# Expert loop: a sixth pair of weight buffers, one result instruction, and a new order of the steps around the weight splits

## The chip, the cores and the metric

One Trainium2 chip, one of its cores, one launch of one program. The metric is the device time of the kernel in microseconds. The engines are called PE (TensorE), DVE (VectorE), ACT (ScalarE), POOL (GpSimd) and SP (SyncE, which only issues DMAs here).

## The reference

One layer of a latent diffusion backbone: 1024 latent tokens and 256 context tokens of width 1024, fp32. Modulated RMSNorm, one combined projection, grouped and differential attention, an output projection with a gated residual; then modulated RMSNorm, a mixture of 32 experts, four for each token, a gated residual and a last RMSNorm. The change is in the experts. For the rows of an expert `e`, with `gate` each row's softmax weight among its four experts, and `gt2` the residual's gate:

```
hcat  = xb @ w_in[e] + b_in[e]                       # 1024 -> 2048
x_glu = min(hcat[:, :1024], 7)
x_lin = clip(hcat[:, 1024:], -7, 7)
act   = x_glu * sigmoid(1.702 * x_glu) * (x_lin + 1)
y     = act @ w_out[e] + b_out[e]                    # 1024 -> 1024
x    += gt2 * sum over a token's experts of gate * y
```

## The kernel before, in words

The program computes modulation, attention and routing in its first 918 us, then runs `stage_e`, the 32 experts, then adds up and normalises. All of it is one unrolled program; each engine works through its own queue in the order in which the code issues the instructions, and waits at an instruction until what that reads or overwrites is ready. The expert stage is issued by hand in a fixed order (`manual_schedule`).

Each expert has up to 128 main rows and up to 64 leftover rows. The products are done in three matmuls on split operands: a weight `w` becomes `wh` (ScalarE's copy, rounded to TensorE's fp32r) and `wl = w - wh` (VectorE), the rows likewise, and `mm3` (lines 87 to 89) adds `xh*wh + xh*wl + xl*wh`. The unit is a weight half, 128 x 1024: two column blocks of 512, so six matmuls. An expert has 16 halves for the input product (`in_mm`, i = 0 to 15, even i for the first 1024 columns of `H`) and eight for the output product (`out_mm`, k = 0 to 7). The split halves lie in a ring of NW = 5 pairs `wh`, `wl` (lines 1197 and 1198): after each half, `split_ahead(1)` issues the split of the half that stands NW places further on in the list `seq`, into the pair that was just used.

PSUM has eight banks: `H` four, `y` two (one tile each), and two ring tiles `r` that serve everything else: the transposes of rows (`columns`, line 1185), of activations (`act_cols`, line 1292), the leftover input (`L[e]`, two of them, blanked by ScalarE at line 1170) and the leftover output. A ring tile is handed on when its last reader is done.

Iteration `e` of the main loop runs in this order:

- issue the gathers of expert e+1 (POOL, main rows and leftovers);
- the input phase, 16 halves. Behind the split that follows a half: `result(e-2)` at i = 1, the activations of e-1 transposed at i = 3, 5, 7 (`act_cols`), the two leftover tiles blanked at i = 11;
- `act_a`: clamp and gelu of `H`'s first half, clamp of its second (lines 1261 to 1263); `left_in`: a branch on the expert's count (line 1225, 1227), and behind it the leftover rows' input product, on raw weights (line 1249); the loads of expert e+1's input weights (SP); `act_l`: clamps of the two leftover tiles (lines 1270, 1271);
- the output phase of expert e-1, eight halves. Behind the split that follows: the rows of e+1 transposed at k = 1 and 3, the leftovers' at k = 4 (`columns`), a blank tile for the leftover output at k = 5, the products of the activation at k = 6 (`act_b`, lines 1277, 1278);
- `left_out`: the leftover output of e-1, behind the same branch; the loads of the output weights of e.

`result` (lines 1338 and 1342) scales each bank of `y` by gate and `gt2` into `o`, the leftovers into `ol`, and POOL scatters them with addition into DRAM (lines 1344, 1349). For the last expert the products come at k = 3 and its activations are transposed at k = 5, 6, 7, since no input phase follows. Lines 1104 and 1114 issue the weight loads; nine buffers of 1 MB hold input rows, four hold output rows.

Of the kernel before, what the change touches and what calls it, by code (L numbers as in the profile page):

```python
# [20 lines left out]
D = 1024  # L21
# [27 lines left out]
class K:  # L49
# [1029 lines left out]
    def stage_e(self):  # L1079
# [4 lines left out]
        with ExitStack() as ctx:  # L1084
# [7 lines left out]
            NW = 5  # L1092
# [25 lines left out]

            def gather(e):
                gather_main(e)  # L1120
                gather_left(e)
# [134 lines left out]
            COLS, KB, ACI, RI, LB, KAB = (1, 3, 4), 5, (3, 5, 7), 1, 11, 6  # L1256

            def act_a(e):
                gm = sp.tile([128, D], F32, name="ga", tag="ga", bufs=1)
                ln = sp.tile([128, D], F32, name="ln", tag="ln", bufs=1)  # L1260
                nc.vector.tensor_scalar(gm, H[e][:, :1024], 7.0, None, op0=OP.min)
                nc.scalar.activation(gm, gm, AF.Gelu_apprx_sigmoid)
                nc.vector.tensor_scalar(ln, H[e][:, 1024:], 7.0, -7.0, op0=OP.min, op1=OP.max)
                A[e] = [gm, ln]

            def act_l(e):
                gm = sp.tile([128, 2, 256], F32, name="gal", tag="gal", bufs=1)
                ln = sp.tile([128, 2, 256], F32, name="lnl", tag="lnl", bufs=1)
                for u in range(2):
                    nc.vector.tensor_scalar(gm[:, u], L[e][u][:, :256], 7.0, None, op0=OP.min)  # L1270
                    nc.vector.tensor_scalar(ln[:, u], L[e][u][:, 256:], 7.0, -7.0, op0=OP.min, op1=OP.max)
                nc.scalar.activation(gm, gm, AF.Gelu_apprx_sigmoid)
                AL[e] = [gm, ln]

            def act_b(e):
                gm, ln, gl, ll = A[e] + AL[e]
                nc.vector.scalar_tensor_tensor(gm, ln, 1.0, gm, op0=OP.add, op1=OP.mult)  # L1277
                nc.vector.scalar_tensor_tensor(gl.rearrange("p u c -> p (u c)"), ll.rearrange("p u c -> p (u c)"), 1.0,
                                               gl.rearrange("p u c -> p (u c)"), op0=OP.add, op1=OP.mult)
# [21 lines left out]
            def out_mm(e, k):  # L1301
                if k == 0:
                    Y[e] = [ps.tile([128, 512], F32, name="y", tag="y", bufs=2) for _ in range(2)]
# [9 lines left out]
            def left_out(e):  # L1313
                ac = ACT[e][2]
                p = Y[e][2]
# [17 lines left out]
            def result(e):  # L1333
                y0, y1, yl = Y.pop(e)
                o = sp.tile([128, D], F32, name="o", tag="o", bufs=1)
                for b, y in enumerate((y0, y1)):
                    c = slice(512 * b, 512 * b + 512)
                    nc.vector.scalar_tensor_tensor(o[:, c], y, self.gm[:, e:e + 1], self.gt2[:, c],  # L1338
                                                   op0=OP.mult, op1=OP.mult)
                ol = sp.tile([128, 2, 256], F32, name="ol", tag="ol", bufs=1)  # L1340
# [45 lines left out]
            columns(0, 1)  # L1386
            for e in range(NE + 1):
                if 0 < e < NE - 1:
                    gather(e + 1)
                for i in range(16 if e < NE else 0):  # L1390
                    in_mm(e, i)
                    if e > 0 or i < 13:
                        split_ahead(1)
                    else:
                        done[1] += 1
                    if i == RI and e > 1:
                        result(e - 2)
                    if i in ACI and e > 0:
                        act_cols(e - 1, ACI.index(i))
                    if i == 0 and e == 0:  # L1400
                        LLS = left_lists()
                    if i == 2 and e == 0:
                        left_lists2(*LLS)
                        gather_left(0)
                        load_out(0, range(2, 4), nc.gpsimd)
                    if i in (9, 10) and e == 0:
                        columns(1, i - 9)
                    if i == 11 and e == 0:
                        columns(0, 2)
                        gather_left(1)  # L1410
                    if i == LB:
                        L[e] = [blank(), blank()]
                if e == NE:
                    result(e - 2)
                if e < NE:
                    act_a(e)
# [5 lines left out]
                if e == 0:  # L1422
                    load_out(0, range(2))
                    act_l(0)
                    split_ahead()
                    columns(1, 2)
                elif e < NE:
                    act_l(e)
                for k in range(8 if e > 0 else 0):
                    out_mm(e - 1, k)  # L1430
                    split_ahead(1)
                    if e < NE:
                        if k in COLS and e + 1 < NE:
                            columns(e + 1, COLS.index(k))
                        if k == (KAB if e < NE - 1 else 3):
                            act_b(e)
                        if e == NE - 1 and k in (5, 6, 7):
                            act_cols(e, (5, 6, 7).index(k))
                    if k == KB:
                        Y[e - 1].append(blank())  # L1440
                if e == 0:
                    act_b(e)
# [174 lines left out]
```

## Time and profile before

| | |
|---|---|
| time, median of 3 runs | 2431.16 us (2431.13 to 2438.26) |
| profiled execution | 2435.69 us, its span 2433.9 us |
| PE busy | 2253.5 us, 93% |
| DVE busy | 1898.0 us, 78% |
| ACT busy | 1507.5 us, 62% |
| POOL busy | 549.8 us, 23% |
| DMA moved | 557.00 MB, mean 229 GB/s |

The expert stage begins at 918 us; its last weight matmul stands near 2395 us. An engine's busy time counts an instruction from its start to its end; instructions of one engine overlap a little, so their pitch (start to start) is shorter than their duration. A matmul's end is modelled, and each lasts longer than its pitch. In a wait, the name behind the arrow is what the profile takes to have ended it; "issue" means that it shows nothing. PEclk is the granted share of TensorE's full clock, 2.4 GHz; the lower level is 1.2 GHz.

### The profile page before, as it was taken

To read this page: it belongs to the slowest core of one execution; us is meant where nothing else is said; L and a number is where in the kernel's file an instruction comes from. 1 tells how busy PE (TensorE), PEld (TensorE's weight loads), DVE (VectorE), ACT (ScalarE), POOL (GpSimd) and SP (SyncE) were. 2 spreads that over 40 slices of the span, in tenths; PEclk is the share of its full clock that TensorE was granted. 3 is DMA by queue.
4 is the path that set the end of the run, shared out by engine and by line. 5 is a ranking of instruction groups with operands and counts; after the bars stand their busy time and mean duration, and the time that the engine had idled before them with its cause. 6 is when DMAs were issued, how large, how long until landed. Compare 5 with 4: busy or idle time off the path is not lost. (4 is left out here: it accounts for less than half of the span.)

```text
span 2433.9 us, 36793 instructions
## 1 busy us (share of the span) xinstructions
PE 2253.5 (93%) x13548; PEld 1760.6 (72%) x13548; DVE 1898.0 (78%) x2987; ACT 1507.5 (62%) x2285; POOL 549.8 (23%) x699
## 2 busy tenths in 40 slices
PE   6999999998999989999999899999999999999993
PEld 3787788887887767776767777667777677677762
DVE  5897067768997768998867898778878888887884
ACT  4321188887887216776656677666667666666762
POOL 3402100001335342221212222122122122122211
PEclk9999999999999988999999999999999999999996
DMA  7546141111003456896878798779779689687875
GB/s 275 186 135 197 58 134 40 35 32 44 23 19 113 170 200 264 331 363 244 331 269 323 268 366 307 289 291 351 270 292 376 247 333 350 248 341 290 303 273 174
DMA packets 133890, 557.00 MB, mean 229 GB/s; under 512 B 18720, under 2 KB 29632, under 8 KB 100880
## 3 DMA queue, kind: packets, MB, share of 16 engines
q1 hardware_dynamic: 103472, 476.21, 51.3%
q0 software_dynamic: 30176, 77.43, 11.4%
q8 instruction: 169, 2.77, 0.5%
q14 instruction: 73, 0.60, 0.1%
HBM read 495.04 MB, written 50.14 MB: 224 GB/s over the span
## 5 line engine op out<-in xcount | busy, mean ns | idle before, releaser
L1197 ACT ACTIVATE wh<-rin 128x1024 fp32r<-128x1024 f32 x520 | 550.4, 1060 | 261.0 <-PE H L89 231.8
L1198 DVE TENSOR_TENSOR wl<-rin,wh 128x1024 fp32r<-128x1024 f32 x520 | 620.0, 1220 | 110.6 <-ACT wh L1197 108.7
L87 PE MATMUL H<-wh,xt 128*128 128x512 f32 x1024 | 415.8, 406 | 0.0
L88 PE MATMUL H<-wl,xt 128*128 128x512 f32 x1024 | 407.8, 398 | 2.7 <-DVE ga L1277 1.5
L89 PE MATMUL H<-wh,xt 128*128 128x512 f32 x1024 | 407.8, 398 | 0.0
L1198 DVE TENSOR_TENSOR wl<-rout,wh 128x1024 fp32r<-128x1024 f32 x248 | 296.4, 1222 | 88.5 <-ACT wh L1197 84.4
L1197 ACT ACTIVATE wh<-rout 128x1024 fp32r<-128x1024 f32 x248 | 256.6, 1054 | 46.8 <-PE H L89 27.3
L89 PEld LDWEIGHTS H<-wh,xt 128*128 128x128 f32 x1024 | 194.7, 190 | 48.8 <-issue 2.6
L88 PEld LDWEIGHTS H<-wl,xt 128*128 128x128 f32 x1024 | 195.1, 191 | 43.5 <-DVE wl L1198 1.0
L87 PEld LDWEIGHTS H<-wh,xt 128*128 128x128 f32 x1024 | 194.9, 190 | 42.6 <-issue 0.7
L87 PE MATMUL y<-wh,at 128*128 128x512 f32 x512 | 210.7, 411 | 0.0
L88 PE MATMUL y<-wl,at 128*128 128x512 f32 x512 | 202.8, 396 | 0.5 <-DVE wl L1198 0.5
L89 PE MATMUL y<-wh,at 128*128 128x512 f32 x512 | 203.1, 397 | 0.0
L1126 POOL DMA_INDIRECT xg<-h2d,im x31 | 33.2, 1070 | 659.4 <-PE r L1185 658.8
L658 ACT ACTIVATE PT<-T 128x512 f32<-128x512 f32 (+1 forms) x256 | 144.8, 573 | 45.5 <-PE T L657 44.6
L657 PE MATMUL T<-ident,P 128*128 128x128 f32 x960 | 147.4, 276 | 9.8 <-DVE P L620 5.5
L1349 POOL DMA_INDIRECT acc<-ol,il x64 | 151.3, 2365 | 17.7 <-DVE wl L1198 15.2
L567 ACT ACTIVATE P<-S,m 128x1024 f32<-128x1024 f32 x128 | 143.4, 1121 | 11.8 <-DVE m L553 6.4
L1344 POOL DMA_INDIRECT acc<-o,im x32 | 51.7, 1615 | 417.3 <-DVE o L1338 385.4
L657 PEld LDWEIGHTS T<-ident,P 128*128 128x128 f32 x960 | 113.0, 141 | 39.6 <-DVE Q L486 9.1
L88 PE MATMUL g<-wl,hh 128*128 128x512 f32 (+1 forms) x368 | 137.4, 373 | 3.5 <-POOL wl L232 3.5
L87 PE MATMUL g<-wh,hh 128*128 128x512 f32 (+1 forms) x368 | 138.8, 377 | 0.5 <-ACT hh L82 0.5
(340 smaller groups left out, 4356.8 us busy)
## 6 DMA issues: line engine op xcount, KB each, us to landing
rin<-in_w_in SPq DMA_DIRECT2D x252, 1024.0 KB
rout<-in_w_out SPq DMA_DIRECT2D x122, 1024.0 KB
ld<-in_w_ada SPq DMA_DIRECT2D x48, 512.0 KB
wr<-in_w_qkv SPq DMA_DIRECT2D x32, 256.0 KB
Q<-Q SPq DMA_DIRECT2D x32, 256.0 KB
xl<-in_x SPq DMA_DIRECT2D x8, 512.0 KB
xr<-in_x SPq DMA_DIRECT2D x8, 512.0 KB
acc<-x POOLq DMA_DIRECT2D x8, 512.0 KB
```

The source lines that it names most:

```text
L87: nc.tensor.matmul(p, ah, bh, start=start, stop=False)
L88: nc.tensor.matmul(p, ah, bl, start=False, stop=False)
L89: nc.tensor.matmul(p, al, bh, start=False, stop=stop)
L567: nc.scalar.activation(parts[k][0], parts[k][1], AF.Exp, bias=m, scale=0.125, accum_out=l2[:, k:k + 1])
L657: nc.tensor.transpose(p[:, k, :], P[:, 128 * j:128 * j + 128], self.ident)
L658: nc.scalar.activation(PT[u - 1][:, 4 * g:4 * g + len(w), :], p[:, :len(w)], AF.Copy)
L1126: nc.gpsimd.indirect_dma_start(out=xg, out_offset=None, in_=self.h2d[:, :], in_offset=bass.IndirectOffsetOnAxis(ap=self.im[:, e:e + 1], ax ...
L1197: nc.scalar.activation(h, src, AF.Copy)
L1198: nc.vector.tensor_tensor(l, src, h.bitcast(F32), op=OP.subtract)
L1344: sc = [nc.gpsimd.indirect_dma_start(out=self.acc[:, :], out_offset=bass.IndirectOffsetOnAxis(ap=self.im[:, e:e + 1], axis=0), in_=o, in_o ...
L1349: i = nc.gpsimd.indirect_dma_start(out=self.acc.rearrange("t (j d) -> (t j) d", j=4), out_offset=bass.IndirectOffsetOnAxis(ap=self.il[:, u ...
```

## The change

Ring of split weights: six pairs instead of five. `y` becomes one tile over two banks, and `result` scales it in one instruction; `o` and `ol` take the slots of `ln` and `lnl`. The steps are cut smaller (`clamp_g`, `gelu`, `clamp_l`, `clamp_left`, `gelu_left`, `act`, `act_left`) and issued by `around_in` and `around_out`, each called before ('<') and after ('>') the split that follows a half:

- input phase: `result` before the split at i = 0, `act_cols` before those at 2, 4, 6; the leftover columns of expert e itself after that at 8, with the leftover gather of e+1 behind them; blanks before that at 9; the clamp of `H`'s first half before the last split, the clamp of the second half behind it;
- output phase: gelu before the split at k = 0, leftover gelu after that at 2, both columns of e+1 before that at 3, the blank after that at 4, the product before that at 6, the leftover product after that at 7. For the last expert both products before that at 3, `act_cols` before those at 5, 6, 7.

```diff
...
             VAL = {}
...
-            NW = 5
+            NW = 6
...
-
-            def gather(e):
-                gather_main(e)
-                gather_left(e)
...
             A, AL = {}, {}
-            COLS, KB, ACI, RI, LB, KAB = (1, 3, 4), 5, (3, 5, 7), 1, 11, 6
-
-            def act_a(e):
+            def clamp_g(e):
                 gm = sp.tile([128, D], F32, name="ga", tag="ga", bufs=1)
+                nc.vector.tensor_scalar(gm, H[e][:, :1024], 7.0, None, op0=OP.min)
+                A[e] = [gm]
+            def gelu(e):
+                nc.scalar.activation(A[e][0], A[e][0], AF.Gelu_apprx_sigmoid)
+            def clamp_l(e):
                 ln = sp.tile([128, D], F32, name="ln", tag="ln", bufs=1)
-                nc.vector.tensor_scalar(gm, H[e][:, :1024], 7.0, None, op0=OP.min)
-                nc.scalar.activation(gm, gm, AF.Gelu_apprx_sigmoid)
                 nc.vector.tensor_scalar(ln, H[e][:, 1024:], 7.0, -7.0, op0=OP.min, op1=OP.max)
-                A[e] = [gm, ln]
-
-            def act_l(e):
+                A[e].append(ln)
+            def clamp_left(e):
                 gm = sp.tile([128, 2, 256], F32, name="gal", tag="gal", bufs=1)
                 ln = sp.tile([128, 2, 256], F32, name="lnl", tag="lnl", bufs=1)
                 for u in range(2):
                     nc.vector.tensor_scalar(gm[:, u], L[e][u][:, :256], 7.0, None, op0=OP.min)
                     nc.vector.tensor_scalar(ln[:, u], L[e][u][:, 256:], 7.0, -7.0, op0=OP.min, op1=OP.max)
-                nc.scalar.activation(gm, gm, AF.Gelu_apprx_sigmoid)
                 AL[e] = [gm, ln]
-            def act_b(e):
-                gm, ln, gl, ll = A[e] + AL[e]
+            def gelu_left(e):
+                nc.scalar.activation(AL[e][0], AL[e][0], AF.Gelu_apprx_sigmoid)
+            def act(e):
+                gm, ln = A[e]
                 nc.vector.scalar_tensor_tensor(gm, ln, 1.0, gm, op0=OP.add, op1=OP.mult)
-                nc.vector.scalar_tensor_tensor(gl.rearrange("p u c -> p (u c)"), ll.rearrange("p u c -> p (u c)"), 1.0,
-                                               gl.rearrange("p u c -> p (u c)"), op0=OP.add, op1=OP.mult)
+            def act_left(e):
+                gl, ll = [x.rearrange("p u c -> p (u c)") for x in AL[e]]
+                nc.vector.scalar_tensor_tensor(gl, ll, 1.0, gl, op0=OP.add, op1=OP.mult)
...
             def out_mm(e, k):
                 if k == 0:
-                    Y[e] = [ps.tile([128, 512], F32, name="y", tag="y", bufs=2) for _ in range(2)]
+                    y = ps.tile([128, 1024], F32, name="y", tag="y", bufs=1)
+                    Y[e] = [y[:, :512], y[:, 512:], y]
                     for b in range(2):
                         nc.tensor.matmul(Y[e][b], sel(e, 1), self.bias[:, 512 + 512 * b:1024 + 512 * b],
                                          start=True, stop=False)
...
             def left_out(e):
-                p = Y[e][2]
+                p = Y[e][3]
...
             def result(e):
-                y0, y1, yl = Y.pop(e)
-                o = sp.tile([128, D], F32, name="o", tag="o", bufs=1)
-                for b, y in enumerate((y0, y1)):
-                    c = slice(512 * b, 512 * b + 512)
-                    nc.vector.scalar_tensor_tensor(o[:, c], y, self.gm[:, e:e + 1], self.gt2[:, c],
-                                                   op0=OP.mult, op1=OP.mult)
-                ol = sp.tile([128, 2, 256], F32, name="ol", tag="ol", bufs=1)
+                y, yl = Y.pop(e)[2:]
+                o = sp.tile([128, D], F32, name="o", tag="ln", bufs=1)
+                nc.vector.scalar_tensor_tensor(o, y, self.gm[:, e:e + 1], self.gt2, op0=OP.mult, op1=OP.mult)
+                ol = sp.tile([128, 2, 256], F32, name="ol", tag="lnl", bufs=1)
                 for u in range(2):
                     nc.vector.scalar_tensor_tensor(ol[:, u], yl[:, 256 * u:256 * u + 256], self.gl[:, u, e:e + 1],
                                                    self.gt2l, op0=OP.mult, op1=OP.mult)
...
+            def around_in(e, i, side):
+                if e == 0:
+                    if (i, side) == (0, '>'):
+                        LLS.extend(left_lists())
+                    if (i, side) == (2, '>'):
+                        left_lists2(*LLS)
+                        gather_left(0)
+                        load_out(0, range(2, 4), nc.gpsimd)
+                    if i in (9, 10) and side == '>':
+                        columns(1, i - 9)
+                    if (i, side) == (11, '>'):
+                        columns(0, 2)
+                        gather_left(1)
+                        L[e] = [blank(), blank()]
+                else:
+                    if (i, side) == (0, '<') and e > 1:
+                        result(e - 2)
+                    if i in (2, 4, 6) and side == '<':
+                        act_cols(e - 1, i // 2 - 1)
+                    if (i, side) == (8, '>'):
+                        columns(e, 2)
+                        if e + 1 < NE:
+                            gather_left(e + 1)
+                    if (i, side) == (9, '<'):
+                        L[e] = [blank(), blank()]
+                if (i, side) == (15, '<'):
+                    clamp_g(e)
+            def around_out(e, k, side):
+                if e < NE:
+                    if (k, side) == (0, '<'):
+                        gelu(e)
+                    if (k, side) == (2, '>'):
+                        gelu_left(e)
+                if e < NE - 1:
+                    if (k, side) == (3, '<'):
+                        columns(e + 1, 0)
+                        columns(e + 1, 1)
+                    if (k, side) == (6, '<'):
+                        act(e)
+                    if (k, side) == (7, '>'):
+                        act_left(e)
+                if e == NE - 1:
+                    if (k, side) == (3, '<'):
+                        act(e)
+                        act_left(e)
+                    if k in (5, 6, 7) and side == '<':
+                        act_cols(e, k - 5)
+                if (k, side) == (4, '>'):
+                    Y[e - 1].append(blank())
+            LLS = []
             for e in range(NE + 1):
                 if 0 < e < NE - 1:
-                    gather(e + 1)
+                    gather_main(e + 1)
                 for i in range(16 if e < NE else 0):
                     in_mm(e, i)
+                    around_in(e, i, '<')
                     if e > 0 or i < 13:
                         split_ahead(1)
                     else:
                         done[1] += 1
-                    if i == RI and e > 1:
-                        result(e - 2)
-                    if i in ACI and e > 0:
-                        act_cols(e - 1, ACI.index(i))
-                    if i == 0 and e == 0:
-                        LLS = left_lists()
-                    if i == 2 and e == 0:
-                        left_lists2(*LLS)
-                        gather_left(0)
-                        load_out(0, range(2, 4), nc.gpsimd)
-                    if i in (9, 10) and e == 0:
-                        columns(1, i - 9)
-                    if i == 11 and e == 0:
-                        columns(0, 2)
-                        gather_left(1)
-                    if i == LB:
-                        L[e] = [blank(), blank()]
+                    around_in(e, i, '>')
                 if e == NE:
                     result(e - 2)
+                if e == 0:
+                    gelu(0)
                 if e < NE:
-                    act_a(e)
+                    clamp_l(e)
                     left_in(e)
                 if e + 1 < NE:
                     load_in(e + 1, range(8) if e else range(2, 8))
...
                     load_out(e)
                 if e == 0:
                     load_out(0, range(2))
-                    act_l(0)
+                    clamp_left(0)
+                    gelu_left(0)
                     split_ahead()
-                    columns(1, 2)
                 elif e < NE:
-                    act_l(e)
+                    clamp_left(e)
                 for k in range(8 if e > 0 else 0):
                     out_mm(e - 1, k)
+                    around_out(e, k, '<')
                     split_ahead(1)
-                    if e < NE:
-                        if k in COLS and e + 1 < NE:
-                            columns(e + 1, COLS.index(k))
-                        if k == (KAB if e < NE - 1 else 3):
-                            act_b(e)
-                        if e == NE - 1 and k in (5, 6, 7):
-                            act_cols(e, (5, 6, 7).index(k))
-                    if k == KB:
-                        Y[e - 1].append(blank())
+                    around_out(e, k, '>')
                 if e == 0:
-                    act_b(e)
+                    act(e)
+                    act_left(e)
                 if e > 0:
                     left_out(e - 1)
                     if e < NE:
```

## Rows read from the trace of the kernel before

**Rows 1.** The page's first part, whole span: busy us, share, instructions.

```profile
PE 2253.5 (93%) x13548; PEld 1760.6 (72%) x13548; DVE 1898.0 (78%) x2987; ACT 1507.5 (62%) x2285; POOL 549.8 (23%) x699
```

**Rows 2.** Windows (length, busy of five engines, PEclk, DMA, GB/s): expert stage, one expert's period.

```profile
...
918.00:2360.00 1442.00, 1375.12 (x7525) 1033.70 (x7524) 1196.01 (x1264) 976.60 (x1103) 322.90 (x249) 0.99 0.82 307
1018.95:1059.21 40.26, 38.22 (x175) 30.33 (x175) 37.70 (x41) 30.73 (x36) 10.94 (x8) 1.00 0.94 353
```

**Rows 3.** Waits of TensorE, 970 to 2340 us: total us, times, longest.

```profile
...
PE r L1185 <- issue: 29.8, 17, 2.0
PE H L1214 <- PEq L1225: 15.8, 6, 3.1
```

**Rows 4.** Timeline of TensorE, end of an expert's input phase and start of outputs.

```profile
...
1435.29 0.40 PE L89 MATMUL H<-wh,xt 128*128 128x512 f32 x1
...
1436.37 0.40 PE L87 MATMUL y<-wh,at 128*128 128x512 f32 x1
...
1438.94 0.40 PE L89 MATMUL y<-wh,at 128*128 128x512 f32 x1
1441.07 0.52 PE L1185 MATMUL r<-ident,xg 128*128 128x128 f32 x3 [1.74 <-issue]
```

**Rows 5.** Timeline of VectorE over the same stretch: start, us, instruction.

```profile
...
1433.20 4.84 DVE L1198 TENSOR_TENSOR wl<-rout,wh 128x1024 fp32r<-128x1024 f32 x4 [0.76 <-ACT wh L1197]
1437.96 1.22 DVE L1261 TENSOR_SCALAR ga<-H 128x1024 f32<-128x1024 f32 x1
1439.09 1.22 DVE L1263 TENSOR_SCALAR ln<-H 128x1024 f32<-128x1024 f32 x1
1440.22 0.41 DVE L1270 TENSOR_SCALAR gal<-r 128x256 f32<-128x256 f32 x1
1440.56 0.41 DVE L1271 TENSOR_SCALAR lnl<-r 128x256 f32<-128x256 f32 x1
```

**Rows 6.** Timeline of VectorE, output phase and next input phase.

```profile
...
1406.98 0.68 DVE L1189 TENSOR_TENSOR xt<-r,xt 128x512 fp32r<-128x512 f32 x1
1407.58 3.48 DVE L1198 TENSOR_TENSOR wl<-rin,wh 128x1024 fp32r<-128x1024 f32 x3
1410.98 1.22 DVE L1277 SCALAR_TENSOR_TENSOR ga<-ln,ga 128x1024 f32<-128x1024 f32 x1
1412.12 0.68 DVE L1278 SCALAR_TENSOR_TENSOR gal<-lnl,gal 128x512 f32<-128x512 f32 x1
...
1417.06 1.40 DVE L1338 SCALAR_TENSOR_TENSOR o<-y,gmain,gt 128x512 f32<-128x512 f32 x2
1418.38 0.86 DVE L1342 SCALAR_TENSOR_TENSOR ol<-r,gleft,gt2l 128x256 f32<-128x256 f32 x2
```

**Rows 7.** Timeline of POOL: the first scatter of one expert's result.

```profile
...
1458.97 1.62 POOL L1344 DMA_INDIRECT acc<-o,im  x1 [8.23 <-DVE o L1338]
```

**Rows 8.** DMA engines' busy tenths, 40 slices of 1.125 us from 1435.

```profile
...
DMA  0389999999999999999999999999999999710000
```

**Rows 9.** Timeline, all engines, between experts 0 and 1.

```profile
...
949.64 1.22 DVE L1263 TENSOR_SCALAR ln<-H 128x1024 f32<-128x1024 f32 x1
...
951.77 0.63 PE L1185 MATMUL r<-ident,xgl 128*128 128x128 f32 x4 [3.31 <-DVE lnl L1271]
...
952.16 0.48 PE L1214 MATMUL H<-bias,selm 128*128 128x512 f32 x1
```

**Rows 10.** Timeline of TensorE, output phase of the last expert's iteration.

```profile
...
2357.92 0.40 PE L87 MATMUL y<-wh,at 128*128 128x512 f32 x1
...
2370.41 1.09 PE L1292 MATMUL r<-ident,ga 128*128 128x128 f32 x4 [3.21 <-DVE ga L1277]
...
2376.70 0.66 PE L1292 MATMUL r<-ident,gal 128*128 128x128 f32 x4 [0.87 <-DVE at L1296]
2377.29 0.64 PE L1319 MATMUL r<-bias,selm 128*32 128x256 f32 x8
```

**Rows 11.** Windows: the 3.5 us behind one wait at line 1185.

```profile
...
2270.00:2273.50 3.50, 3.50 (x12) 2.79 (x13) 2.19 (x3) 3.48 (x5) 0.00 (x0) 0.61 1.01 428
```

## The prediction

> **What bounds the kernel now.** I read the page's busy shares first: TensorE is busy for 93% of the span and VectorE for 78% [rows 1]. The table by windows then separates the expert stage: 1442 us long, TensorE busy for 1375 us at a granted clock of 0.99, DMA share 0.82 [rows 2]. So the stage is bound by TensorE, and only what makes TensorE wait can be won. The waits of TensorE in the steady part (experts 1 to 30) are short to list: 29.8 us in 17 waits before the transposes `r` of line 1185, 15.8 us in six waits at a branch (line 1225), and little else [rows 3].
>
> The 17 are labelled "issue", so the timeline has to say what they wait for. Call T the end of an expert's last `H` matmul: the last one starts at 1435.29, matmuls follow each other every 0.23, so T = 1435.52 [rows 4]. Eleven pitches take 2.57 us (1436.37 to 1438.94), so one weight half (six matmuls) is 1.40. The first `y` half starts at T+0.85; two halves end at T+3.65, and there TensorE wants the transposes of the next expert's rows. They start at 1441.07, T+5.55: 1.90 us late. VectorE's timeline shows why [rows 5]. Four weight splits queued earlier run until 1438, then the clamps of `H` (`ga`, `ln`), then the clamps of the first leftover bank, of which the last ends at 1440.56 + 0.41 = 1440.97. The transposes need that `r` bank, and start 0.10 us later. So it is a wait for VectorE's queue. It comes in the experts without leftover rows; with them TensorE has the work of line 1249 in between.
>
> **The change, part by part.** Columns from k = 1, 3, 4 to k = 3 (both halves), ahead of that step's split, and the leftover third to i = 8 of the next input phase. TensorE now reaches the first transposes after four halves, T + 0.85 + 5.60 = T+6.45. Today's bank release, T+5.45, would already be in time. The clamp of `H`'s first half is also issued ahead of the last split instead of behind it, and six buffers let ScalarE and VectorE run further ahead. I walk VectorE's queue with the starts-to-starts of its rows: split 1.13 (three from 1407.58 to 1410.98), `ga` and `ln` 1.13 each, a leftover clamp 0.33, a transposed half (`xt`, `at`) 0.60, the product `ga` 1.14, the small one, as wide as a transposed half, 0.60, both `ol` 0.8 [rows 5, 6]. If VectorE has caught up by then, its split of half 14 ends at about T+0.9; then `ga` to 2.0, the split of half 15 to 3.1, `ln` to 4.3, first leftover bank to 5.0, second to 5.6. TensorE wants them at T+6.45 and about T+6.9. The wait of 1.90 us goes, 17 times: **32.3 us**.
>
> What is late next? VectorE has 24 splits (27.1), `H` clamps 2.3, leftover clamps 1.3, products 1.7, four transposed halves 2.4, and results 1.9: 36.7 us for each expert. TensorE's period without the wait is 40.26 - 1.90 = 38.36 us [rows 2]. VectorE fits, with 1.6 us to spare, but its work bunches in the output phase, so I walk on. After T+5.6 come the splits of k0 to k2 (to T+9.0), two `xt` (10.2), splits k3 to k5 (13.6), `ga` (14.7), splits k6, k7 (17.0), the small product (17.6), `o` and `ol` (19.5), then the splits of the next input phase with two `at` among them: i0 ready at 20.7, i1 21.8, i2 23.5, i5 27.5, caught up near i12 at 35. With six buffers the split issued after a half is used six halves later. TensorE, at 1.40 a half, 0.85 at the start of each phase and 0.4 for a group of transposes (952.16 - 951.77 [rows 9]), ends the output phase at T+12.9 and input half 0 at T+15.1; it reaches the half that needs i0's split (half 6) at T+23.4 and the one that needs i1's at T+25.3: 2.7 us to spare at the tightest. With five buffers each would be wanted one half (1.40) earlier, and 1.3 us would be left; that is what the sixth buffer buys. I take no new wait.
>
> Result in one instruction. The two take 1.32 us from start to start of what follows [rows 6]; one over 1024 columns lies between 1.14 (the product `ga`, same width and kind) and 1.32 (no gain). VectorE saves 0 to 0.2 us for each expert, off the path: 0; I take 1.14. The tile `y` is now released as one, a period before its next use. `o` and `ol` now share slots with `ln` and `lnl`, so the clamps wait for the result's scatter to have left SBUF. Today the first scatter of an expert is issued on POOL at 1458.97 [rows 7], and the DMA engines fall quiet near 1474 [rows 8]: all three landed within 15 us. After the change `o` is ready at T+18.7 and `ln` is written at T+38.4+3.1, 22.8 us later. Cost 0; if the landing took longer, each us over would hold VectorE for one.
>
> POOL and DMA. The leftover gather moves behind the result's scatters; it has until the next i = 8, some 30 us. Weight loads begin about 1.6 us after T (1437) and end near 1474 [rows 8]: 36.6 us of a 38.4 us period. That fits, by 1.8 us. Twelve loads in 36.6 us are 3.05 each: with one of the eight input loads there from before, the next lands at about T+4.7, the last at T+23; their first splits issue after k4 (T+8.7) and i8 (T+28). So I take 0 and keep the DMA limit as a rival. If that cover were gone, ScalarE would wait for rows, and TensorE only after the lead of six halves, 8.4 us, is used up.
>
> First expert. The transposes of line 1185 at 951.77 waited 3.31 us for `lnl`; `H` for expert 1 started at 952.16 [rows 9]. With them gone, `H` waits for `ln`, which ends at 949.64 + 1.22 = 950.86: 1.2 us earlier, less 0.4 for the transposes done later: **0.8 us**.
>
> Last expert. TensorE waits before `r<-ident,ga` at 2370.41 and before the third transposes at 2376.70; the leftover output begins at 2377.29 [rows 10]. The first `y` half starts at 2357.92, which is T+0.85, so T = 2357.07. After the change both products stand ahead of the split of k = 3: by the same walk `ga` ends at T+10.2 = 2367.3, and the first transposes start then (today 2370.41). The second wait for `at`, behind the splits k3 and k4, until T+13.7 = 2370.7; with one more half and the third transposes the leftover output begins at 2373.1: **4.2 us**.
>
> Clock. One of the 17 waits was longer (2.0 against a mean of 1.75 [rows 3]); it ended at 2269.9, and in the 3.5 us behind it the granted clock was 0.61 [rows 11], part of it at the lower level, 1.2 GHz. 0.39 x 3.5 = 1.4, and 0.2 for the wait: **1.6 us**.
>
> Sum: 32.3 + 0.8 + 4.2 + 1.6 = 38.9 us. The profiled execution took 2435.69 us (span 2433.9), so 2396.8 there; it lies 4.5 us above the median, 2431.16. From the median: 2392.
>
> **Rivals.**
> 1. *VectorE becomes the bound.* If its instructions did not overlap, the 24 splits at 1.22 (29.3) and the rest at full durations (10.8) make 40.1 us, today's period: nothing is won in the steady part, 2431 - 5 = 2426. Against it: the pitch of 1.13 [rows 6]. The Trainium skill, "VectorE: DVE Perf Modes", section "The DRAIN you can't avoid", says that the next operation doesn't start until the pipe has emptied; by that the time would be this rival's. The trace disagrees: a start every 1.13 us under durations of 1.22.
> 2. *Part of the wait moves.* The walk has 1.4 us to spare at the first transposes and 2.7 at the splits; if the queue is 2.4 us later than walked, half of each wait remains: 17 x 0.95 = 16, so 2408.
> 3. *The weight loads become the bound.* DMA share 0.94 of 40.26 is 37.8, and 1.6 before the loads start: 39.4 us a period, 0.8 won each: 14 + 7 at the ends, 2410. For it: nearly full already; against: loads have slack before their splits.
> 4. *Slower: skipped branches.* Line 1225 jumps over the leftover output where there is none. Six of these jumps cost TensorE 15.8 us, 2.6 each [rows 3]; a stall of that size also brings the slow clock (another 1.4). The code between branches shifts by the moved transposes. If all 18 skipped output branches stalled, 12 more x 4.0 = 48, so 2392 + 48 = 2440; from 10 more on it is slower than today. Against it: the number of TensorE instructions hardly changes, so a handful either way is likelier. The Trainium skill, "Runtime: NRT & Kernel Launch", section "Instruction fetch mechanics", says that a taken branch whose target lies outside the fetched pages waits for a fetch; which branches these are no row here tells.
> 5. *It doesn't do what it says*: the clamps stay behind splits and the wait is something else; no change, 2431.
>
> **How the numbers follow.** Forecast 2392: 0.66, its own range 2384 to 2400 (two of the six branch stalls more or fewer). Rival 2: 0.13, rival 3: 0.08, rival 1: 0.05, rival 4: 0.05, rival 5: 0.03. A measurement of this kernel tells about 0.3%, 7 us, from no change. Faster by more: 0.66 + 0.13 + 0.08 + 0.02 (rival 1 in part) = 0.89; within: 0.03 of rival 1 and 0.03 of rival 5, 0.06; slower: 0.05. The range 2379 to 2418 holds the forecast, rivals 2 and 3, and below it a few branch stalls that vanish.
>
> **What would show it.** TensorE's waits at line 1185 gone in experts without leftovers, and their period 38.4 us instead of 40.26; VectorE busy near 96% of it; no TensorE wait for `wl`, and none of ScalarE for a DMA. Waits of TensorE for `wl` near i = 6 would speak for rivals 1 or 2, waits of ScalarE for `rin` for rival 3, more and longer waits behind the branch for rival 4. A period of 40 us would make the forecast wrong.

## The result and the profile after

The changed kernel takes 2401.06 us (median of four runs, 2396.79 to 2401.89) beside 2433.36 us for the one before (four runs, 2431.13 to 2438.26): ratio 0.9855, 95% interval 0.984 to 0.987. The profiled execution took 2400.34 us, its span is 2398.6. The forecast was 2392 us.

The page's first part, whole span (busy us, share, instructions), against [rows 1]:

```profile
PE 2246.6 (94%) x13548; PEld 1761.0 (73%) x13548; DVE 1895.1 (79%) x2955; ACT 1496.6 (62%) x2285; POOL 525.3 (22%) x699
```

TensorE's busy time falls by only 6.9 us: nearly all of the gain is waiting that is gone. The windows of the expert stage and of one expert's period, columns as in [rows 2]:

```profile
...
918.00:2360.00 1442.00, 1397.55 (x7701) 1055.10 (x7700) 1215.87 (x1262) 980.51 (x1121) 304.31 (x256) 0.99 0.83 309
1021.22:1059.54 38.32, 38.03 (x174) 30.41 (x175) 37.29 (x40) 30.50 (x36) 12.38 (x8) 1.00 0.99 371
```

The period is 38.32 us (40.26 before). VectorE is busy for 37.29 of it, 97%, and the DMA share is 0.99. TensorE still sets the pace, with 0.3 us idle.

Waits of TensorE, 970 to 2340 us, in total, times and the longest, against [rows 3]:

```profile
...
PE y L1310 <- PEq L1221: 6.8, 4, 2.7
PE y L1310 <- PEq L1223: 5.5, 12, 0.5
PE H L1210 <- PEq L1223: 5.1, 11, 0.5
PE H L1210 <- PEq L1221: 4.6, 3, 2.5
PE H L88 <- DVE ga L1279: 1.7, 1, 1.7
...
```

The 17 waits before the transposes (29.8 us) have no successor. Seven branch waits of 11.4 us together, five of them above 1 us, stand where six of 15.8 were (line 1221 is the old 1225). TensorE's timeline at the end of that period, against [rows 4]:

```profile
...
1059.00 0.40 PE L89 MATMUL H<-wh,xt 128*128 128x512 f32 x1
1059.54 0.70 PE L1310 MATMUL y<-bias,selm 128*128 128x512 f32 x2
1060.08 0.40 PE L87 MATMUL y<-wh,at 128*128 128x512 f32 x1
...
1065.43 0.40 PE L89 MATMUL y<-wh,at 128*128 128x512 f32 x1
1065.66 1.04 PE L1181 MATMUL r<-ident,xg 128*128 128x128 f32 x8
```

VectorE's over the same stretch, against [rows 5]:

```profile
...
1059.12 1.23 DVE L1194 TENSOR_TENSOR wl<-rout,wh 128x1024 fp32r<-128x1024 f32 x1 [0.17 <-ACT wh L1193]
1060.27 1.22 DVE L1255 TENSOR_SCALAR ga<-H 128x1024 f32<-128x1024 f32 x1
1061.40 1.22 DVE L1194 TENSOR_TENSOR wl<-rout,wh 128x1024 fp32r<-128x1024 f32 x1
1062.53 1.22 DVE L1263 TENSOR_SCALAR ln<-H 128x1024 f32<-128x1024 f32 x1
1063.67 0.41 DVE L1270 TENSOR_SCALAR gal<-r 128x256 f32<-128x256 f32 x1
1064.00 0.41 DVE L1271 TENSOR_SCALAR lnl<-r 128x256 f32<-128x256 f32 x1
...
```

T is 1059.23. VectorE frees the first bank at 1064.41 = T+5.18, and TensorE comes for it at T+6.43, straight behind a matmul.

To place the whole difference I cut both traces at the same matmuls: the first transposes of line 1181 (1185 before), and the bias matmuls that open the first, the second-last and the last `y`.

| part, us | before | after | difference | forecast |
|---|---|---|---|---|
| ahead of the first transposes | 917.24 | 918.33 | +1.1 | 0 |
| to the first `y` (first expert) | 61.45 | 64.61 | +3.2 | -0.8 |
| to the second-last `y` (steady part) | 1378.69 | 1336.41 | -42.3 | -33.9 |
| to the last matmul (last expert) | 35.94 | 38.37 | +2.4 | -4.2 |
| behind it | 40.6 | 40.9 | +0.3 | 0 |
| span | 2433.9 | 2398.6 | -35.3 | -38.9 |

The steady part's gain splits further. Branch waits fell by 4.8 us (15.8 + 0.4 to 11.4). Stretches at 1.2 GHz fell from six, 20.5 us in all, to three, 10.2 us; they run at half speed, so half of the difference, 5.1 us, is won. That leaves 32.4 us for the 17 waits. It is a remainder, but the one period above fell by 1.94 us, and 17 x 1.94 is 33.0. The steady part is 1336.66 and 1335.41 us in two more profiles of the changed kernel; the kernel before has only the one profile.

The end is where the changed kernel loses. TensorE's timeline of the last output phases, against [rows 10]:

```profile
...
2329.56 0.63 PE L1296 MATMUL r<-ident,ga 128*128 128x128 f32 x4 [1.16 <-DVE ga L1279]
...
2332.95 0.66 PE L1296 MATMUL r<-ident,ga 128*128 128x128 f32 x4 [1.38 <-DVE at L1300]
...
2335.02 0.66 PE L1296 MATMUL r<-ident,gal 128*128 128x128 f32 x4
2335.61 0.64 PE L1324 MATMUL r<-bias,selm 128*32 128x256 f32 x8
2336.06 3.64 PE L1331 MATMUL r<-rout,ac 128*32 128x256 f32 x64
2343.91 1.22 PE L1310 MATMUL y<-bias,selm 128*128 128x512 f32 x2 [4.21 <-DVE o L1341]
```

ScalarE's, from 2334 us:

```profile
...
2339.86 0.60 ACT L1302 ACTIVATE ac<-r 128x512 f32<-128x512 f32 x1 [4.67 <-PEq L1223]
2340.35 1.05 ACT L1193 ACTIVATE wh<-rin 128x1024 fp32r<-128x1024 f32 x1
```

VectorE's, the same stretch:

```profile
...
2341.43 1.23 DVE L1194 TENSOR_TENSOR wl<-rin,wh 128x1024 fp32r<-128x1024 f32 x1 [4.99 <-ACT wh L1193]
2342.57 1.28 DVE L1341 SCALAR_TENSOR_TENSOR o<-y,gmain,gt 128x1024 f32<-128x1024 f32 x1
...
```

Read the three from the bottom. TensorE waits for `o` to read the old `y`; `o` stands on VectorE behind the split `wl`; that needs ScalarE's `wh`, which stands behind the copy `ac`; and the copy may overwrite the old `ac` only after the leftover output (line 1331) has read it. One step, now issued ahead of the split at k = 7, has put three queues in series. The clock falls during the wait and stays low behind it (columns as in [rows 2]; the first 1.9 of these 7 us still belong to the wait):

```profile
...
2342.00:2349.00 7.00, 5.09 (x12) 4.03 (x13) 2.82 (x5) 1.06 (x1) 4.34 (x5) 0.51 0.43 67
```

### The profile page after: what moved, and what is told of

It reads as the page before. It is cut to its first block, busy times and chain, and to the rows that moved or that the text cites. A ratio compares the mean times of both kernels' runs of the same rounds, so it can differ in the third digit from the quotient of the medians.

```text
span 2398.6 us, 36791 instructions
## 1 busy us (share of the span) xinstructions
PE 2246.6 (94%) x13548; PEld 1761.0 (73%) x13548; DVE 1895.1 (79%) x2955; ACT 1496.6 (62%) x2285; POOL 525.3 (22%) x699
## 5 line engine op out<-in xcount | busy, mean ns | idle before, releaser
L1193 ACT ACTIVATE wh<-rin 128x1024 fp32r<-128x1024 f32 x520 | 535.3, 1056 | 171.9 <-PE H L89 139.7
L1194 DVE TENSOR_TENSOR wl<-rout,wh 128x1024 fp32r<-128x1024 f32 x248 | 298.9, 1221 | 47.1 <-ACT wh L1193 45.1
L89 PE MATMUL g<-wh,xl 128*128 128x512 f32 (+1 forms) x368 | 137.3, 373 | 0.5 <-DVE xl L83 0.5
L1130 POOL DMA_INDIRECT xgl<-h2d,il x64 | 87.0, 1360 | 229.3 <-PE r L1181 195.7
```

The source lines that it names most:

```text
L89: nc.tensor.matmul(p, al, bh, start=False, stop=stop)
L1130: nc.gpsimd.indirect_dma_start(out=xl[:, u, :], out_offset=None, in_=self.h2d.rearrange("t (j d) -> (t j) d", j=4), in_offset=bass.Indirec ...
L1193: nc.scalar.activation(h, src, AF.Copy)
L1194: nc.vector.tensor_tensor(l, src, h.bitcast(F32), op=OP.subtract)
```

## The experiments

**The columns' move, in the old code: alone, then with the third.** First theory: the new places of the transposes are what removes the 17 waits.

```diff
-                        if k in COLS and e + 1 < NE:
-                            columns(e + 1, COLS.index(k))
+                        if k == 3 and e + 1 < NE:
+                            columns(e + 1, 0)
+                            columns(e + 1, 1)
+                        if k == 4 and e + 1 < NE:
+                            columns(e + 1, 2)
```

> The kernel before with one step moved: both columns of expert e+1 at k = 3 of the output phase (behind the split, as before), instead of k = 1 and k = 3; five buffers, two result instructions, the clamps still behind the splits. Theory (place): the bank of the first leftover tile is free at T+5.45 in any case, TensorE now comes at T+6.45, so all 17 waits at the transposes go, the period of an expert without leftovers falls from 40.26 to 38.4 us, and the time is 2433 - 34 = 2399, without losses at the start or the end of the stage (no wait of TensorE for cp, none for o). Rival (order): the clamps have to be issued ahead of the splits as well; VectorE falls behind without the pause, the wait comes back at k = 3 with half its size or more, 17 x 0.95 = 16 us, and the time is 2415 or above.

Measured: 2502.88 us, 1.0273 (1.0256 to 1.029) of before. The waits list of TensorE, 970 to 2340 us:

```profile
...
PE r L1185 <- DVE xt L1189: 75.1, 29, 3.9
...
```

A miss on every side: the old wait is gone, but the third group, one weight half behind the other two, needs a ring tile that VectorE's `xt` has still to read, and `xt` is queued behind the splits. TensorE waits 75.1 us for it, and 82 us of the steady part run at 1.2 GHz (20.5 before). So the third group must move as well; the next kernel does that in the old code, where everything still stands behind the split.

```diff
-                gather(e + 1)
+                gather_main(e + 1)
...
+                    if i == 8 and e > 0:
+                        columns(e, 2)
+                        if e + 1 < NE:
+                            gather_left(e + 1)
...
-                    columns(1, 2)
...
-                        if k in COLS and e + 1 < NE:
-                            columns(e + 1, COLS.index(k))
+                        if k == 3 and e + 1 < NE:
+                            columns(e + 1, 0)
+                            columns(e + 1, 1)
```

> The kernel before with all three groups of columns where the change has them (both halves at k = 3, the leftover third at i = 8 of the next input phase with the leftover gather behind it), each behind the split; five buffers, two result instructions, clamps and everything else as before. Theory (place): the leftover third no longer waits for a ring tile that VectorE's xt still reads, and the first transposes come after the clamps: no waits of TensorE at the transposes, period 38.4 us, 2434 - 38 = 2396 at best, 2402 at worst. Rival (order): with the clamps still behind the splits the waits at k = 3 come back, 17 x 0.5 us or more, 2410 or above.

Measured: 2421.43 us, 0.9939 (0.9917 to 0.9962). Waits of TensorE, 970 to 2340 us:

```profile
...
PE H L1214 <- PEq L1225: 16.1, 5, 4.4
PE H L1214 <- PEq L1227: 7.0, 11, 2.3
PE H L1214 <- issue: 5.7, 2, 3.7
...
PE r L1319 <- ACT r L1170: 4.7, 8, 0.6
PE r L1292 <- DVE ol L1342: 1.8, 2, 0.9
...
PE y L1305 <- PEq L1225: 1.2, 2, 0.9
```

The 17 waits are gone: the move of all three groups does that by itself. The steady part, 1361.25 us, is 17.4 shorter than before, although branches cost 8.7 more (16.1 + 5.7 + 1.2, and 1.9 beyond the usual 0.46 each in the second row: 24.9 against 16.2) and 6.5 go into the two rows that wait for ring tiles. Without these two losses it would be 32.6 shorter, which is again what the 17 waits are worth. The 5.7 labelled "issue" are counted as branch waits because they stand ahead of the `H` of experts 5 and 22, where other profiles name the branch; that is a reading.

The changed kernel is 24.8 us ahead of this one: 13.5 at branches (24.9 against 11.4), 5.1 at the low clock (20.5 us against 10.2) and the 6.5. Only those 6.5 can be put down to the rest of the new order, blanks included, since their two rows are missing from the changed kernel's list.

**The first transposes back at k = 1 in the changed kernel.**

```diff
-                    if (k, side) == (3, '<'):
+                    if (k, side) == (1, '<'):
                         columns(e + 1, 0)
+                    if (k, side) == (3, '<'):
                         columns(e + 1, 1)
```

> The changed kernel with the first columns back at k = 1 (ahead of the split) and the second at k = 3; all else as changed. Theory (place): TensorE wants the bank at T+3.65 and VectorE, with the clamp of H ahead of the last split, frees it at T+5.2: 17 waits of about 1.5 us, 26 us in all, time 2401 + 26 = 2427. Rival (order): the earlier clamp alone does it, no waits at the transposes, 2401.

Measured: 2419.83 us, 0.9932 (0.9916 to 0.9949). Waits of TensorE, 970 to 2320 us:

```profile
...
PE r L1181 <- issue: 21.1, 15, 1.5
...
```

The wait is back, in 15 experts and 1.41 us each. That the bank clears only after TensorE wants it at k = 1 is thereby shown from both sides; with the clamp ahead of the split the wait is 0.34 shorter than before (1.75). The time is 18 us above the changed kernel's and not 26 as expected: 21.1 us of waits came back, but only 3.4 us of the steady part run at 1.2 GHz, against 10.2.

**The sixth buffer: taken out of the changed kernel, and alone in the old one.**

```diff
-            NW = 6
+            NW = 5
```

> The changed kernel with NW = 5. Theory (the sixth buffer is slack only): no wait of TensorE for wl in the steady part, period 38.4 us as with six; at the start VectorE has one split less ahead of cp, so the wait of TensorE for cp (3.38 us) and most of the slow clock behind it (6.83 us at half rate, 3.4 us) go: 2401 - 6 = 2395. Rival (the sixth buffer carries the gain): with 1.4 us less lead TensorE waits for wl in each of the 17 experts without leftovers, 0.3 us or more each, and the time is 2401 or above.

Measured: 2401.38 us, 0.985 (0.9834 to 0.9867), the changed kernel's ratio. Its list has no wait for `wl`. Its steady part is 6.9 us longer (1343.29), and 3.5 more at branches (14.9) and a longer stay at 1.2 GHz (17.0 us) account for that. The other way round, with `NW = 6` in the kernel before and its `o` and `ol` in the slots of `ln` and `lnl`:

```diff
-            NW = 5
+            NW = 6
...
-                o = sp.tile([128, D], F32, name="o", tag="o", bufs=1)
+                o = sp.tile([128, D], F32, name="o", tag="ln", bufs=1)
...
-                ol = sp.tile([128, 2, 256], F32, name="ol", tag="ol", bufs=1)
+                ol = sp.tile([128, 2, 256], F32, name="ol", tag="lnl", bufs=1)
```

> The kernel before with six pairs of weight halves (o and ol in the slots of ln and lnl, to make room), the order of all steps as before. Theory (order): the same splits still stand ahead of the clamps in VectorE's queue, so the 17 waits at line 1185 stay, 1.9 us each; at the start TensorE waits about 1 to 3 us for cp; time as before or up to 7 us more. Rival (depth): with one pair more VectorE comes to the clamps earlier, the waits shrink to below 1 us, and the time is 2420 or less.

Measured: 2445.1 us, 1.0029 (1.0016 to 1.0043). Waits of TensorE, 970 to 2340 us:

```profile
...
PE r L1185 <- DVE lnl L1271: 30.6, 17, 1.9
...
```

The 17 waits stay, and here the trace names VectorE's `lnl`, which had to be inferred from the timelines when the label was "issue". The sixth buffer by itself is worth nothing; its small loss comes together with a longer stay at 1.2 GHz (40.9 us against 20.5).

**The result in two instructions again, in the changed kernel.**

```diff
-                nc.vector.scalar_tensor_tensor(o, y, self.gm[:, e:e + 1], self.gt2, op0=OP.mult, op1=OP.mult)
+                for b in range(2):
+                    c = slice(512 * b, 512 * b + 512)
+                    nc.vector.scalar_tensor_tensor(o[:, c], y[:, c], self.gm[:, e:e + 1], self.gt2[:, c],
+                                                   op0=OP.mult, op1=OP.mult)
```

> The changed kernel with the result scaled in two instructions of 512 columns again (y stays one tile over two banks). Theory (off the path): VectorE works 0.2 us more for each expert and TensorE's waits stay as they are: within 2 us of the changed kernel, 2401. Rival (VectorE is the bound now): 0.2 us for each of 31 experts, 6 us, 2407.

Measured: 2399.14 us, 0.9841 (0.9821 to 0.9861); the changed kernel in the same comparison 2400.44, 0.9848. No difference: the one instruction takes 1.278 us, the two 0.743 each with overlap, and VectorE is off the path.

**Both ends mended.** The list transposes of the first expert later, and the last expert's copy `ac` behind the result that frees `y`.

```diff
-                    if (i, side) == (2, '>'):
+                    if (i, side) == (5, '>'):
                         left_lists2(*LLS)
...
-                    if k in (5, 6, 7) and side == '<':
+                    if k in (5, 6) and side == '<':
                         act_cols(e, k - 5)
...
                     result(e - 2)
+                    act_cols(e - 1, 2)
```

> The changed kernel with two steps moved back: the transposes of the leftover lists at i = 5 of the first input phase instead of i = 2, and the third transposes of the last expert's activation behind result(30) instead of ahead of the split at k = 7. Theory (two waits at the ends ate part of the gain): the wait of TensorE for cp (3.38 us) and the one for o (4.21 us) go, and with each 6.83 us at half clock (3.4 us): 14 us, 2401 - 14 = 2387. Rival (they are hidden by the next wait): the list transposes make the first expert's leftover columns late, or the last output still waits for the branch, and less than half is won: 2394 or above.

Measured: 2400.35 us (2391.48 to 2402.17), 0.985 (0.9834 to 0.9867): no gain to be told, though the profiled execution, at 2391.48, was the fastest of the four. So both kernels were timed side by side, twice.

> The changed kernel once more, unaltered, as the measure for the next one. Theory (the waits at skipped branches are fixed by where the code lies): the same branches stall as in its first trace (before H of experts 10 and 26, before y of iterations 10, 15 and 26), with lengths between 1.3 and 3.5 us; time 2401. Rival (they fall at random): other branches stall, and their number differs by two or more.

> The changed kernel with the two steps at the ends moved (list transposes at i = 5 of the first input phase; the last third of the last expert's activation behind result(30)), beside the changed kernel in the same job. Theory (two waits ate part of the gain): 9 us less than the changed kernel, as its trace showed (start to first H 37.1 to 34.5, the last two output phases 38.4 to 32.1 us): about 2392 beside 2401. Rival (its first timing, where three of four runs lay at 2399 to 2402): within 3 us of the changed kernel, and then the two waits came back somewhere else in those runs.

> The changed kernel, unaltered, as the measure for the next one in the same job: 2400 us.

> The changed kernel with both ends moved, timed a third time, since its first two timings differ (2400.35 and 2392.54). Theory (two waits at the ends): 6 to 10 us below the changed kernel in the same job. Rival (no lasting gain): within 3 us of it.

Measured: the changed kernel 2400.44 us (0.9848, 0.9833 to 0.9863), with both ends mended 2392.54 (0.981, 0.9795 to 0.9825); then 2398.33 (0.9843, 0.9825 to 0.9861) and 2395.69 (0.9834, 0.9818 to 0.9851). The first pair's intervals stand apart, the second pair's overlap. The traces are firmer: from second-last to last `y` is 24.55 to 24.56 us in three profiles of the changed kernel and 20.55 to 20.56 in three of this one. TensorE's timeline of the mended end, in the second of the three:

```profile
...
2335.43 3.64 PE L1331 MATMUL r<-rout,ac 128*32 128x256 f32 x64
2339.53 0.66 PE L1296 MATMUL r<-ident,gal 128*128 128x128 f32 x4 [0.47 <-PEq L1223]
2339.95 0.71 PE L1310 MATMUL y<-bias,selm 128*128 128x512 f32 x2
```

The wait of 4.21 us is gone, the bias matmuls take 0.71 instead of 1.22, and the end takes 32.0 to 32.1 us instead of 38.3 to 38.4. That is also 3.9 less than the 35.94 of the kernel before. Moving the list transposes is a wash: from the first transposes to the second expert's `H` it is 34.47, 37.57 and 34.44 us with them late, 37.14, 34.88 and 34.87 without. With them late TensorE no longer waits for the lists, but for the gathered leftover rows that depend on them: 0.9, 2.7 and 1.0 us for `xgl`. Side by side the mended kernel is 7.9 and 2.6 us below the changed one, and only the 7.9 stands clear of the noise. Why its first timing showed nothing stays open: the three runs at 2399 to 2402 us have no trace.

**Branch stalls: the kernel with both ends mended, its code shifted.** 32 transposes whose result nobody reads stand ahead of the first expert (64 TensorE instructions with their weight loads).

```diff
             columns(0, 1)
+            pad = ring()
+            for _ in range(32):
+                nc.tensor.transpose(pad[:, :128], self.ident, self.ident)
```

> The changed kernel with both ends moved, and 32 transposes of the identity that nothing reads added after the first expert's columns, so that all later TensorE code lies 64 instructions further on (cost 32 x 0.11 = 3.5 us). Theory (a skipped branch stalls where the code lies so): the stalls above 1.2 us at branches leave H of experts 10 and 26 and y of iterations 10, 15 and 26 and come at others, and their number changes by one or more. Rival (they belong to these experts): the same five stall; time 2392 + 3.5 = 2396 in that case.

Measured: 2396.95 us, 0.9824 (0.9793 to 0.9854). In the three profiles of the changed kernel and the three of its mended form the long branch waits stand ahead of `H` of experts 10 and 26 and ahead of `y` of experts 10, 15 and 26; here they stand ahead of `H` of 6, 11, 22 and 28 and of `y` of 17 and 28. The places moved with the code, which speaks for its position as the cause. One shift does not prove it: two versions with the same matmuls in the same order and another number of buffers (in one also other tile slots) differ too (a stall of 3.09 us ahead of `H` of expert 4 with five buffers; `H` of 11, 22 and 28 with the sixth alone, which the kernel before does not have). Which lengths of code stall, and whether one avoids them all, stays open.

## Why the prediction was right, and where not

- **The 17 waits.** Forecast 32.3 us, 32.4 left as the remainder. VectorE's walk gave the bank at T+5.0 and the want at T+6.45; the rows show 5.18 and 6.43. Columns back at k = 1 brings the waits back, moving all the columns in the old code removes them. TensorE's list has no row for line 1181, so no part of the wait moved (rival 2 falls), and the change does what it says (rival 5 falls).
- **VectorE fits** (rival 1 falls): 97% busy in a period of 38.32, against 96% and 38.36 forecast. `ga`, `wl` and `ln` in the rows above start 1.13 apart under durations of 1.22. The Trainium skill's rule that the next operation starts only when the pipe is empty ("VectorE: DVE Perf Modes", section "The DRAIN you can't avoid") would by itself have them 1.22 apart, and this trace disagrees. The same section adds that a next operation that is not held starts earlier; the prediction left that out, and the 1.13 is in keeping with it.
- **The sixth buffer and the DMA** (rival 3 falls): five buffers run the same time, as the 1.3 us of slack left with five had it. The DMA share reached 0.99 without a ScalarE wait for a load among the eight longest in its list.
- **The result in one instruction**: nothing, as forecast.
- **Clock and branches**, forecast 1.6 us: measured 5.1 and 4.8. The stretch behind the wait of [rows 11] lasted 3.4 us and cost 1.7; the window of those rows ends inside it and gave 1.4. The branch stalls were put at no change, and they changed in the kernel's favour. The rival in which more of them stall was the right thing to price, with the wrong sign here. The Trainium skill's rule that a taken branch out of the fetched pages waits for a fetch ("Runtime: NRT & Kernel Launch", section "Instruction fetch mechanics") is in keeping with the shifted code, in which the stalls moved; no trace here shows a fetch.
- **The first expert**, forecast 0.8 gained, measured 3.2 lost; the two other profiles of the same kernel lose 0.9 and 1.0. TensorE's last wait ahead of the second expert's `H` did shrink, from 3.31 to 2.54. But the copy of the lists is queued on VectorE behind the splits, and the wait for it grew from 0.2 us to 3.4 (1.3 and 1.9 in the two other profiles). With five buffers that wait was absent and this part was as short as before (61.29), so it is the sixth split ahead of the copy that costs it (with the sixth buffer alone in the old code the wait is 1.7). The forecast put no cost on that.
- **The last expert: the step that failed.** The forecast has "the leftover output begins at 2373.1", T+16.0, and it began at T+16.6: that much nearly came true. What failed stands earlier: "The tile `y` is now released as one, a period before its next use", costed at nothing. In the last iteration the next use follows the leftover output at once, and `o`, which releases `y`, waits through two queues for the copy `ac`. The walk followed VectorE alone; ScalarE's copy, moved ahead of a split, was not counted. It cost 4.21 us and the low clock behind it: 2.4 lost where 4.2 gained were forecast. With that one copy moved back behind the result, the part is 3.9 us shorter than before, so the rest of the walk held.
- **The size.** Between the profiled executions 35.3 us were won against 38.9 forecast: 8.4 more than forecast in the steady part, 12.0 less at the ends and outside the experts. That is 3.6 of the 9 us between 2392 and 2401.06; most of the rest is the starting point, since the profiled execution lay 4.5 above the median from which the forecast was taken. That median, 2431.16 us in three runs, was low: 2433.36 in four, and 2436 to 2439 in the later comparisons. Against those the changed kernel's gain is 37 to 40 us (2437.15 to 2400.44, 2438.17 to 2398.33). The 2401.06 lies just above the forecast's own range, 2384 to 2400, and inside the whole one, 2379 to 2418.

## What to carry to other kernels

When a consumer is moved later so that a slower engine can finish, walk every in-order queue that it is moved past: the third transposes left one half behind the others cost 67 us net, a copy ahead of one split 4.2. Walk the first and the last iteration by themselves, since a release that lies a whole period ahead in the steady part can be the very next thing at the end. A buffer or a merged instruction that only adds slack where nobody waits is worth nothing, and a deeper queue of splits can delay what stands behind it, as the sixth did for the lists.

## What was not expected of the hardware

A branch wait can bring the low clock with it. TensorE's timeline and the window behind its wait (columns as in [rows 2]), changed kernel:

```profile
...
2062.73 0.40 PE L89 MATMUL y<-wh,at 128*128 128x512 f32 x1
2065.63 0.74 PE L1210 MATMUL H<-bias,selm 128*128 128x512 f32 x1 [2.50 <-PEq L1221]
```

```profile
...
2065.70:2069.10 3.40, 3.40 (x8) 2.69 (x9) 3.40 (x5) 0.00 (x0) 0.00 (x0) 0.50 1.03 423
```

TensorE did nothing for 2.50 us; behind it the granted clock is 0.50, that is 1.2 GHz, for 3.40 us, which costs another 1.7. So it went behind the waits of 2.70 and 2.50 us in this trace, and not behind those of 1.42, 1.89 and 1.99. The stalls themselves, 1.2 to 3.2 us in the six profiles of the changed kernel and its mended form, keep their places from one profile to the next and lengthen or shorten there. The stage ahead of the experts, whose code the change leaves alone, ended between 917.2 and 923.1 us.
